# The first 100 microseconds of a hybrid decoder step: a new order of the first loads, and a written order on ACT and DVE

## The chip, the cores and the metric

The kernel runs on one core of a Trainium2 chip. The engines are TensorE (PE), VectorE (DVE), ScalarE (ACT), GpSimd (POOL) and SyncE (SP); nearly every transfer of this kernel is issued from SP's queue, in order. The metric is the device time of one execution in microseconds, the median over runs.

## The reference

One inference step of a one-layer decoder with two mixers side by side. A prompt of 2048 rows and 64 sample rows (8 sequences of 8), each 1024 wide, are normalised and projected by one weight matrix:

```python
h = rmsnorm(x, norm_w)
z = h @ w_in
q, k, v, qb, kb, vb, g_lr, gate_a, gate_b = jnp.split(z, split_points(), axis=-1)
q = rope(rmsnorm(heads(q, H_A), q_norm_w), pos)
k = rope(rmsnorm(heads(k, H_A), k_norm_w), pos)
o_a = attend(q, k, v)            # mixture of (window, dilation) = (128,1), (512,4), (2048,16)
log_a = log_sigmoid(g_lr @ w_gate_up + b_gate) / 16
o_b, s_fin = gla_chunked(qb * 64 ** -0.5, kb, vb, log_a, s0)
o_b = rmsnorm(o_b, gla_norm_w)
y = x + concat([o_a * silu(gate_a), o_b * silu(gate_b)]) @ w_out
```

8 attention heads of 64, 4 linear-attention heads. Outputs are y for prompt and sample, the new keys and values, and the final states. All inputs are float32.

## The kernel before, in words

**Numbers as pairs.** PE multiplies float16 pairs. A row tile of the prompt (128 rows) is normalised and split into a high and a low half; so is each block of weights, after scaling by powers of two. A product is then three matmuls for each of 8 slices of 128 input columns: 24 matmuls of 128x512 for each tile and block.

**The first rows.** `fetch(t)` loads x of tile t (512 KB). `prep(t)` squares it on ACT (L520), takes the inverse root with small operations on DVE and ACT (`rsqrt`, L117), writes the high half on ACT (L528) and the low half on DVE (L529), has SP transpose both by a transposing transfer (L532, into `hl`), and stores the transposed tile for later use (L536, into `h_d`). The sample rows (`prep("s")`) are transposed on PE instead (L543). Tiles 0 to 3 have input buffers of their own.

**The first weights.** `load_w(name)` is a generator. Its first step issues eight loads of 256 KB into four paired buffers of the pool `wr` (tag "wr", 4 buffers; x of tiles 4 and up uses the same tag). Eight steps take the maximum (block v: on DVE, L603; the others: a sum of squares on ACT, L608). One step brings it to a scale (`spread_max` with two small PE products, L569 and L572, then DVE). The last eight steps write the high part on ACT (L635) and the low part on DVE (L636). `between` and `behind` name rows that are fetched after half or all of the eight loads. `at_once` runs a generator to its end.

**The order.** The program calls, as traced before: fetch of the sample rows, all of `load_w("v")` with tile 0's x between its loads and tiles 1 to 3 behind, `prep("s")`, `prep(0)` to `prep(3)`; then the small tables (L1001 to L1044: `nwo` for the output weights, the masks `m3w` and `m3c`, the tables `tabs` of the two head norms with their scales `scl`); then `first(0)`. `first(0)` projects v for the sample and tiles 0 to 3, then q, then k; it calls `load_w("q")` after v's tile 0 and `load_w("k")` after v's tile 3. The projected rows are evacuated from PSUM by ACT and DVE (`post`: L736 and L744, L745 for v; L662, L663 for q and k) and, for q and k, worked on by POOL (`qk_post`, L687 to L693, with the tables of L679). Two PSUM banks (`ps_Y`) hold the sums; `vs` has two buffers (tag "z2"), `vp` one. Later blocks of rows (`first(1)` to `first(3)`) are woven with attention work. `scores_of` lists steps that read the sample's cached keys (`sample_keys`, L956) and multiply them on POOL.

**Who decides the order of an engine.** The framework records the calls and plans the order of the instructions on each engine at build time, from an estimated timeline; calls recorded earlier come first where both could run. Each engine then runs its list strictly in order. Waits for data and for buffers are added by the framework. `tc.issue_after(ins)` adds an order without a wait: each instruction recorded in the block that runs on the engine (or queue) of `ins` is placed behind `ins` in that engine's list. A buffer of a pool is given again when its last reader is done.

Of the kernel before, what the change touches and what calls it, by code (L numbers as in the profile page):

```python
# [7 lines left out]
F32 = mybir.dt.float32  # L8
# [4 lines left out]
AF = mybir.ActivationFunctionType  # L13
ALU = mybir.AluOpType
AX = mybir.AxisListType
# [3 lines left out]
P = 128  # L19
D = 1024  # L20
KT = D // P
# [12 lines left out]
Q_SCALE = 2.0**14  # L34
# [18 lines left out]
def tile_hymba(ctx: ExitStack, tc: tile.TileContext, A: dict):  # L53
# [318 lines left out]
    with ExitStack() as c1:  # L372
# [132 lines left out]
        def prep(t):  # L505
            again[0] += 1
            n = NS if t == "s" else P
            u = again[0]
            x = xs.pop(t)[:]
            wide = t != "s" and t > 3  # L510
            as_x = lambda ap: ap.rearrange("p (a c) -> p a c", a=2) if wide else ap
            if t == "s":
                hs = hps.tile([P, KT, 2 * NS], F16, name="hs")
                hi, lo = hs[:, :, 0:NS], hs[:, :, NS:]
            else:
                hl = hp.tile([P, 2, KT, n], F16, name=f"hl_{u}", tag="hl")
# [3 lines left out]
            ACT.activation(as_x(jk[:n]), x[:n], AF.Square, accum_out=ss[:n])  # L520
            rs = sm.tile([P, 1], F32, name=f"rs_{u}", tag="rs")
            rsqrt(sm, rs[:n], ss[:n], 1.0 / D, n, 1, f"x{u}", H_SCALE)
            if t != "s":
                if t < 4:
                    ht = early_ht[:, t]
                else:
                    ht = xp.tile([P, 2, D], F16, name=f"ht_{u}", tag="ht", bufs=1)[:]
                ACT.activation(as_x(ht[:, 0]), x, AF.Copy, scale=rs[:])  # L528
                DVE.scalar_tensor_tensor(  # L529
                    as_x(ht[:, 1]), x, rs[:], as_x(ht[:, 0]), ALU.mult, ALU.subtract  # L530
                )
                SP.dma_start_transpose(  # L532
                    hl[:].rearrange("p a k c -> p (a k) c"), ht.rearrange("p a c -> p (a c)")
                )
                hT[t] = (hi, lo)
                SP.dma_start(h_d[t * P : (t + 1) * P, :], hl[:].rearrange("p a k c -> p (a k c)"))  # L536
# [37 lines left out]
            )  # L574
            return pt[:, P : P + 1]

        loaded, powers = {}, {}

        def load_w(name, between=(), behind=()):

# [6 lines left out]
            for k in range(KT):  # L587
                if k % 2 == 0:
                    pair = wr.tile([P, 2, 528], F32, name=f"wr_{name}_{k}", tag="wr")
                raw = pair[:, k % 2]  # L590
                SP.dma_start(raw[:, :n], src[k * P : (k + 1) * P, c0 : c0 + n])
# [40 lines left out]
            w = wp.tile([P, 2, KT, 528], F16, name=f"w_{name}", tag="w")  # L632
            for k in range(KT):
                h, l = w[:, 0, k, :n], w[:, 1, k, :n]
                ACT.activation(h, raws[k][:, :n], AF.Copy, scale=nws[:, k : k + 1])  # L635
                DVE.scalar_tensor_tensor(  # L636
                    l, raws[k][:, :n], nws[:, k : k + 1], h, ALU.mult, ALU.subtract
                )
                yield
            loaded[name] = (w, inv)  # L640
# [2 lines left out]
        def at_once(gen):  # L643
            for _ in gen:
                pass
# [356 lines left out]
        DVE.memset(nwo[:, 0:4], 1.0)  # L1002
        for k in range(4, KT):
            SP.dma_start(nwo[:, k : k + 1], A["gla_norm_w"][0].rearrange("(k p) -> p k", p=P))
        m3w = at1.tile([P, 384], F32, name="m3w")
        SP.dma_start(m3w[:], A["c_m3"])
        m3c = at1.tile([P, 384], F32, name="m3c")
        POOL.tensor_scalar(
            m3c[:].rearrange("p (b c j) -> p b c j", c=4, j=32),
            m3w[:].rearrange("p (b j c) -> p b c j", c=4, j=32), 1e-10, None, ALU.mult,  # L1010
        )

        DVE.tensor_scalar(m3w[:], m3w[:], 1e-10, None, ALU.mult)
# [6 lines left out]
        for nm_, src in (("q", A["q_norm_w"]), ("k", A["k_norm_w"])):  # L1020
            i = "qk".index(nm_)
            w = tabs[:, 0, i]
            SP.dma_start(w, src.to_broadcast([P, 64]))
            for half in range(2):
                SP.dma_start(
                    tabs[:, 1, i, 32 * half : 32 * half + 32],
                    src[:, 32 - 32 * half : 64 - 32 * half].to_broadcast([P, 32]),
                )
            pw = scl[nm_]
            DVE.tensor_reduce(pw[:], w, AX.X, ALU.max, apply_absolute_value=True)  # L1030
            DVE.tensor_scalar(pw[:], pw[:], 2.0**-8, None, ALU.max)
            power(pw[:], pw[:])
        DVE.tensor_tensor(scl["s"][:], scl["q"][:], scl["k"][:], ALU.mult)
        DVE.tensor_scalar(scl["s"][:], scl["s"][:], -1.0 / (Q_SCALE * K_SCALE), None, ALU.mult)
        for n_, c_ in (("q", Q_SCALE), ("k", K_SCALE)):
            DVE.reciprocal(scl[n_][:], scl[n_][:])
            DVE.tensor_scalar(scl[n_][:], scl[n_][:], c_, None, ALU.mult)

        for i in range(2):
            DVE.tensor_scalar(  # L1040
                tabs[:, i, 0], tabs[:, i, 0], scl["q"][:], 0.125, ALU.mult, ALU.mult
            )
        unq = kp.tile([P, 1], F32, name="unq")
        DVE.reciprocal(unq[:], scl["q"][:])  # L1044

        kk = ap_.tile([P, NH, 4, 2, P], F16, name="kk", tag="kk", bufs=1)

# [909 lines left out]
```

## Time and profile before

| | |
|---|---|
| median of three runs | 1352.06 us (1351.25 to 1354.95) |
| the profiled execution's own time | 1347.42 us |
| its span, first to last instruction | 1345.6 us |
| mean granted TensorE clock | 0.979 |
| PE busy | 1218.3 us, 91% |
| DVE, ACT, POOL busy | 933.1, 878.8, 641.6 us |
| PE busy in 0 to 25, 25 to 60, 60 to 85 us | 3.78, 28.80, 22.65 us |
| transfers | 285.27 MB, mean 212 GB/s |
| cached keys, one load | 256.0 KB |

A row of the timeline gives start, duration, engine, line, operation, output and inputs, and the count of like instructions that it merges. In square brackets stands how long the engine had been idle before it and what ended that. A row of SPq is the issue of a transfer, not the transfer itself; when it landed is seen from who waited for it.

### The profile page before, as it was taken

What the parts mean: (1) busy time and instruction counts of PE and PEld (TensorE: products, weight loads), DVE (VectorE), ACT (ScalarE), POOL (GpSimd) and SP (SyncE); (2) the same over time, 40 slices, a digit from 0 to 9 for tenths busy, and PEclk for the clock granted to TensorE, in tenths of its full rate; (3) what the DMA queues carried; (4) which work ended last, traced back from release to release, by engine and by line L of the source; (5) the groups of instructions that cost most, each with busy time, mean ns of one, the idle gap of its engine ahead of it and who ended that gap; (6) DMA issues with size and microseconds to landing.
All of it is one profiled execution on the core that took longest, in us unless ns stands there. A gap on an engine that the chain in (4) does not pass through costs nothing.

```text
span 1345.6 us, 26148 instructions
## 1 busy us (share of the span) xinstructions
PE 1218.3 (91%) x8878; PEld 722.5 (54%) x8878; DVE 933.1 (69%) x2266; ACT 878.8 (65%) x2331; POOL 641.6 (48%) x597
## 2 busy tenths in 40 slices
PE   3798999988899798998999998789999999999998
PEld 1343565555566555665766565556655544444443
DVE  6367767788677968767771769977564387787842
ACT  5655787778568877788994557655776475465520
POOL 0076554878678645651115756777440033332310
PEclk9999999999999999999999998989999999999999
DMA  8859857778957599969886355455335768998952
GB/s 259 243 162 260 233 162 161 203 203 216 238 167 207 174 278 274 299 183 220 215 190 196 85 165 199 144 168 157 98 111 190 275 197 302 376 325 312 351 200 83
DMA packets 251721, 285.27 MB, mean 212 GB/s; under 512 B 125426, under 2 KB 160195, under 8 KB 251587
## 3 DMA queue, kind: packets, MB, share of 16 engines
q1 hardware_dynamic: 251586, 283.60, 70.7%
q8 instruction: 70, 1.15, 0.4%
q14 instruction: 65, 0.52, 0.1%
HBM read 183.12 MB, written 75.24 MB: 192 GB/s over the span
## 4 chain that ended last, share of the span: by engine, by line
PE 35%; DVE 20%; DMA 17%; POOL 10%; issue 9%; ACT 6%; SPq 3%; POOLq 0%; DVEq 0%; ACTq 0%
PE Y L1579 5%; DVE qbd L243 3%; PE acc_vb L1105 3%; PE acc_qkb L1105 3%; POOL pr L951 3%; PE acc_gb L1105 3%; PE O L467 2%; PE acc_g L1105 2%; PE s L434 2%; PE t L452 2%; DMA v<-vp_d 2%; DMA qb<-q_d 2%; PE acc_q L1105 2%; PE acc_k L1105 2%; POOL pt L419 2%
## 5 line engine op out<-in xcount | busy, mean ns | idle before, releaser
L1105 PEld LDWEIGHTS <-hr 128*128 128x128 f16 x1824 | 174.5, 99 | 133.1 <-issue 21.6
L951 POOL TENSOR_TENSOR pr<-k,qb 128x512 f32<-128x512 f32 x128 | 176.5, 1379 | 115.8 <-DVE sck L952 79.7
L445 ACT ACTIVATE p<-p,o 128x256 f32<-128x256 f32 (+1 forms) x384 | 173.2, 455 | 53.3 <-DVE o L442 49.4
L1105 PEld LDWEIGHTS <-hl 128*128 128x128 f16 x1248 | 122.4, 100 | 152.3 <-issue 26.2
L1579 PE MATMUL Y<-w_o,mh 128*128 128x512 f16 x768 | 177.5, 381 | 3.5 <-ACT mh L1538 3.4
L419 POOL TENSOR_TENSOR pt<-p,pt 128x512 f16<-128x512 f32 (+1 forms) x80 | 94.4, 1180 | 145.7 <-ACT pt L418 126.1
L1621 POOL TENSOR_TENSOR tc<-oc,w 128x512 f32<-128x512 f32 x32 | 49.0, 1550 | 178.7 <-DVE w L1613 169.5
L467 PE MATMUL O<-v,pt 128*128 128x128 f16 x1200 | 110.3, 220 | 25.1 <-DMA v<-vp_d 7.9
L1579 PEld LDWEIGHTS <-mh 128*128 128x128 f16 x768 | 71.9, 98 | 91.4 <-issue 8.8
L952 DVE TENSOR_REDUCE sck<-pr 128x8 f32<-128x512 f32 x128 | 87.0, 680 | 48.9 <-POOL pr L951 48.5
L452 PE MATMUL t<-ident,p 128*128 128x128 f32 x600 | 105.4, 279 | 5.0 <-ACT p L445 3.0
L467 PEld LDWEIGHTS <-pt 128*128 128x128 f16 x1200 | 81.9, 98 | 51.8 <-POOL pt L419 12.0
L1105 PE MATMUL acc_v<-w_v,hl 128*128 128x512 f16 x384 | 95.2, 391 | 8.5 <-DVE vp L745 3.5
L442 DVE CUSTOM_DVE_ANT_0 p<-s,m3w,scl_s 128x128 f32<-128x128 f32 (+1 forms) x256 | 89.0, 394 | 17.2 <-POOL pt L419 6.0
L1105 PE MATMUL acc_g<-w_g,hr 128*128 128x272 f16 (+1 forms) x768 | 99.2, 277 | 0.0
L1105 PE MATMUL acc_vb<-w_vb,hr 128*128 128x512 f16 x384 | 96.3, 397 | 1.4 <-ACT zg L719 1.4
L1105 PE MATMUL acc_q<-w_q,hl 128*128 128x512 f16 x384 | 93.1, 392 | 4.1 <-ACT zs_k L663 3.4
L235 ACT ACTIVATE E<-D_e 128x256 f32<-128x256 f32 (+1 forms) x168 | 67.8, 418 | 44.4 <-DVE qbd L243 16.9
L1105 PE MATMUL acc_k<-w_k,hl 128*128 128x512 f16 x384 | 91.2, 383 | 2.1 <-ACT zs_k L663 1.6
L1105 PE MATMUL acc_gb<-w_gb,hr 128*128 128x512 f16 x384 | 88.4, 385 | 3.0 <-ACT zgb L728 3.0
L434 PE MATMUL s<-kk,qq 128*128 128x256 f16 (+1 forms) x512 | 79.6, 269 | 9.5 <-DMA kk<-kp_d 4.8
L227 POOL TENSOR_TENSOR D_e<-b_e 128x512 f32<-128x512 f32 x56 | 66.4, 1196 | 23.2 <-ACT E L235 11.0
(508 smaller groups left out, 2598.2 us busy)
## 6 DMA issues: line engine op xcount, KB each, us to landing
k<-in_cache_k_win SPq DMA_DIRECT2D x104, 256.0 KB
sv<-in_cache_v_win SPq DMA_DIRECT2D x24, 1024.0 KB
hr<-h_d SPq DMA_DIRECT2D x44, 512.0 KB
qb<-q_d SPq DMA_DIRECT2D x64, 256.0 KB
o_d<-o SPq DMA_DIRECT2D x96, 132.0 KB
oc<-o_d SPq DMA_DIRECT2D x48, 264.0 KB
x<-in_x_prompt SPq DMA_DIRECT2D x16, 512.0 KB
h_d<-hl SPq DMA_DIRECT2D x16, 512.0 KB
```

Of the source, the lines that this page charges most:

```text
L227: POOL.tensor_tensor(dv, bv, bv[:, :, 0:1, B - 1 : B].to_broadcast([P, M, 2, B]), ALU.subtract)
L235: ACT.activation(ev[rows, i], dv[rows, :, half, :], AF.Exp, scale=(2 * half - 1) / 16.0)
L419: POOL.tensor_tensor(l, f, h, ALU.subtract)
L434: PE.matmul(s_ps[:, i * w : (i + 1) * w], q, k, start=(n == 0), stop=(n == len(prods) - 1),)
L442: DVE.tensor_tensor_reduce(s[:, sl], s_ps[:, sl], mask, neg, BIG, ALU.add, ALU.min, nmf(i))
L445: ACT.activation(s[:, sl], s[:, sl], AF.Exp, bias=nmf(i), scale=-1.0, accum_out=denf(i))
L452: PE.transpose(p_ps[:, i * P : (i + 1) * P], t["s"][:, i * P : (i + 1) * P], ident[:])
L467: PE.matmul(o_, t["pt"][:, c, (i * nb + b) * P : (i * nb + b + 1) * P], vf(i, b), start=(n == 0), stop=(n == 2 * nb - 1),)
L951: POOL.tensor_tensor(pr[:], kt, qt, ALU.mult)
L952: DVE.tensor_reduce(out, pr[:].rearrange("p (u k d) -> p u k d", u=2, k=4), AX.X, ALU.add)
L1105: PE.matmul(z, a_[:, k, :], w[:, p_, k, cols], start=(k == 0 and i == 0), stop=(k == KT - 1 and i == 2),)
L1579: PE.matmul(Y[:], a_[:, k, :], w_[:, part, k, :512], start=(i == 0), stop=(i == len(prods) - 1),)
```

## The change

All of it is in the first phase.

- Tile 0's x is fetched behind all eight loads of w_v, not after four of them.
- `load_w("v")` is run up to its scale; then `prep("s")` and `prep(0)` are recorded, then two of the eight weight parts, then the other six, which have to follow tile 0's halves on ACT and on DVE. `prep(1)` to `prep(3)` have to follow the last weight part on ACT and on DVE.
- The loads of w_q have to follow tile 0's transpose in SP's queue.
- The small tables are recorded after `load_w("q")`, and have to follow its last load in SP's queue. The head tables are loaded into a buffer of the pool `wr` (`tw`) and written to `tabs` by DVE (two more copies). `nwo` moves to the second block of rows, behind w_k's loads.
- The sample's cached keys are loaded behind w_k's loads.

```diff
@@ prep
-                ACT.activation(as_x(ht[:, 0]), x, AF.Copy, scale=rs[:])
-                DVE.scalar_tensor_tensor(
-                    as_x(ht[:, 1]), x, rs[:], as_x(ht[:, 0]), ALU.mult, ALU.subtract
-                )
-                SP.dma_start_transpose(
+                last["ht"] = (
+                    ACT.activation(as_x(ht[:, 0]), x, AF.Copy, scale=rs[:]).ins,
+                    DVE.scalar_tensor_tensor(
+                        as_x(ht[:, 1]), x, rs[:], as_x(ht[:, 0]), ALU.mult, ALU.subtract
+                    ).ins,
+                )
+                last["turned"] = SP.dma_start_transpose(
                     hl[:].rearrange("p a k c -> p (a k) c"), ht.rearrange("p a c -> p (a c)")
-                )
+                ).ins
@@ load_w
+                last["raw"] = SP.dma_start(raw[:, :n], src[k * P : (k + 1) * P, c0 : c0 + n]).ins
...
+                last["w"] = (
+                    ACT.activation(h, raws[k][:, :n], AF.Copy, scale=nws[:, k : k + 1]).ins,
+                    DVE.scalar_tensor_tensor(
+                        l, raws[k][:, :n], nws[:, k : k + 1], h, ALU.mult, ALU.subtract
+                    ).ins,
                 )
@@ scores_of
-                    sample_keys(*todo[i])
+                    with tc.issue_after(last["raw_k"]):
+                        sample_keys(*todo[i])
@@ the start
         fetch("s")
-        at_once(load_w("v", [0], [1, 2, 3]))
+        parts = load_w("v", (), [0, 1, 2, 3])
+        for _ in range(KT + 1):
+            next(parts)
         prep("s")
-        for t in range(4):
-            prep(t)
+        prep(0)
+        for _ in range(2):
+            next(parts)
+        with ExitStack() as rows0:
+            for i_ in last["ht"]:
+                rows0.enter_context(tc.issue_after(i_))
+            at_once(parts)
+        turned0 = last["turned"]
+        with ExitStack() as split_v:
+            for i_ in last["w"]:
+                split_v.enter_context(tc.issue_after(i_))
+            for t in range(1, 4):
+                prep(t)
...
+        def output_rows():
+            DVE.memset(nwo[:, 0:4], 1.0)
+            for k in range(4, KT):
+                SP.dma_start(nwo[:, k : k + 1], A["gla_norm_w"][0].rearrange("(k p) -> p k", p=P))
+        def mask_tables():
+            SP.dma_start(m3w[:], A["c_m3"])
...
+        def head_tables():
+            tw = wr.tile([P, 2, 528], F32, name="tw", tag="wr")[:, 0, :256].rearrange(
+                "p (s i d) -> p s i d", s=2, i=2
+            )
...
+            for i in range(2):
+                DVE.tensor_scalar(
+                    tabs[:, i, 0], tw[:, i, 0], scl["q"][:], 0.125, ALU.mult, ALU.mult
+                )
+                DVE.tensor_copy(tabs[:, i, 1], tw[:, i, 1])
+            DVE.reciprocal(unq[:], scl["q"][:])
@@ first, m == 0
                             if t == 0:
-                                at_once(load_w("q"))
+                                with tc.issue_after(turned0):
+                                    at_once(load_w("q"))
+                                with tc.issue_after(last["raw"]):
+                                    head_tables()
+                                    mask_tables()
                             elif t == 3:
                                 at_once(load_w("k", (), [4, 5, 6]))
+                                last["raw_k"] = last["raw"]
@@ first, m == 1
             if m == 1:
+                with tc.issue_after(last["raw_k"]):
+                    output_rows()
```

More of the change, by code (lines that the diff above doesn't have):

```diff
@@ L575, in spread_max @@
             return pt[:, P : P + 1]
-        loaded, powers = {}, {}
+        loaded, powers, last = {}, {}, {}
         def load_w(name, between=(), behind=()):
@@ L590, in load_w @@
                 raw = pair[:, k % 2]
-                SP.dma_start(raw[:, :n], src[k * P : (k + 1) * P, c0 : c0 + n])
+                last["raw"] = SP.dma_start(raw[:, :n], src[k * P : (k + 1) * P, c0 : c0 + n]).ins
                 raws.append(raw)
@@ L634, in load_w @@
                 h, l = w[:, 0, k, :n], w[:, 1, k, :n]
-                ACT.activation(h, raws[k][:, :n], AF.Copy, scale=nws[:, k : k + 1])
-                DVE.scalar_tensor_tensor(
-                    l, raws[k][:, :n], nws[:, k : k + 1], h, ALU.mult, ALU.subtract
+                last["w"] = (
[3 more added lines that the diff above has]
+                    ).ins,
                 )
@@ L1019, in tile_hymba @@
         scl = {n_: kp.tile([P, 1], F32, name=f"scl_{n_}") for n_ in "qks"}
[L1020 to L1027, printed above, removed]
-                )
[L1029 to L1042, printed above, removed]
@@ L1043, in tile_hymba @@
-        unq = kp.tile([P, 1], F32, name="unq")
-        DVE.reciprocal(unq[:], scl["q"][:])
+        unq = kp.tile([P, 1], F32, name="unq")
+        def output_rows():
[4 more added lines that the diff above has]
+            SP.dma_start(m3w[:], A["c_m3"])
+            POOL.tensor_scalar(
+                m3c[:].rearrange("p (b c j) -> p b c j", c=4, j=32),
+                m3w[:].rearrange("p (b j c) -> p b c j", c=4, j=32), 1e-10, None, ALU.mult,
+            )
+            DVE.tensor_scalar(m3w[:], m3w[:], 1e-10, None, ALU.mult)
@@ new lines, in head_tables @@
+        def head_tables():
+            tw = wr.tile([P, 2, 528], F32, name="tw", tag="wr")[:, 0, :256].rearrange(
+                "p (s i d) -> p s i d", s=2, i=2
+            )
+            for nm_, src in (("q", A["q_norm_w"]), ("k", A["k_norm_w"])):
+                i = "qk".index(nm_)
+                w = tw[:, 0, i]
+                SP.dma_start(w, src.to_broadcast([P, 64]))
+                for half in range(2):
+                    SP.dma_start(
+                        tw[:, 1, i, 32 * half : 32 * half + 32],
+                        src[:, 32 - 32 * half : 64 - 32 * half].to_broadcast([P, 32]),
+                    )
+                pw = scl[nm_]
+                DVE.tensor_reduce(pw[:], w, AX.X, ALU.max, apply_absolute_value=True)
+                DVE.tensor_scalar(pw[:], pw[:], 2.0**-8, None, ALU.max)
+                power(pw[:], pw[:])
+            DVE.tensor_tensor(scl["s"][:], scl["q"][:], scl["k"][:], ALU.mult)
+            DVE.tensor_scalar(scl["s"][:], scl["s"][:], -1.0 / (Q_SCALE * K_SCALE), None, ALU.mult)
+            for n_, c_ in (("q", Q_SCALE), ("k", K_SCALE)):
+                DVE.reciprocal(scl[n_][:], scl[n_][:])
+                DVE.tensor_scalar(scl[n_][:], scl[n_][:], c_, None, ALU.mult)
+            for i in range(2):
+                DVE.tensor_scalar(
+                    tabs[:, i, 0], tw[:, i, 0], scl["q"][:], 0.125, ALU.mult, ALU.mult
+                )
+                DVE.tensor_copy(tabs[:, i, 1], tw[:, i, 1])
+            DVE.reciprocal(unq[:], scl["q"][:])
```

8 lines of the change are left out of this document (removed).

## The prediction

> **What bounds the kernel now.** I read the page's busy shares first.
>
> ```profile
> PE 1218.3 (91%) x8878; PEld 722.5 (54%) x8878; DVE 933.1 (69%) x2266; ACT 878.8 (65%) x2331; POOL 641.6 (48%) x597
> ```
>
> TensorE is the bound, with 127 us idle in a span of 1345.6. The change works at the start; the table of stretches says how much is at stake there.
>
> ```profile
> 0.00:25.00 25.00, 3.78 (x14) 1.88 (x14) 14.08 (x54) 16.36 (x34) 1.98 (x8) 1.00 0.75 232
> 25.00:60.00 35.00, 28.80 (x114) 12.09 (x115) 17.93 (x38) 19.15 (x40) 0.95 (x1) 0.95 0.91 266
> 60.00:85.00 25.00, 22.65 (x98) 9.77 (x97) 12.33 (x22) 15.65 (x35) 11.06 (x18) 0.93 0.58 180
> 85.00:145.00 60.00, 52.29 (x234) 22.94 (x233) 41.78 (x65) 33.10 (x68) 44.65 (x64) 0.97 0.91 230
> ```
>
> Columns: PE, PEld, DVE, ACT, POOL busy, granted clock, DMA share, GB/s. Up to 85 us PE idles 29.8 us, 21.2 of them before 25. Next the timeline of PE: where it waits, and for what.
>
> ```profile
> 25.46 1.89 PE L1105 MATMUL acc_v<-w_v,hl 128*128 128x512 f16 x4 [0.92 <-DMA hl<-early_ht]
> 33.83 0.81 PE L779 MATMUL acc_v_s<-w_v,hs 128*128 128x512 f16 x3
> 38.15 5.35 PE L1105 MATMUL acc_v<-w_v,hl 128*128 128x512 f16 x24 [2.22 <-DMA hl<-early_ht]
> 52.73 7.03 PE L1105 MATMUL acc_v<-w_v,hl 128*128 128x512 f16 x24 [3.52 <-DVE vp L745]
> 85.19 5.34 PE L1105 MATMUL acc_k<-w_k,hl 128*128 128x512 f16 x24
> ```
>
> Tile 0 starts at 25.46 and shares PE with the sample's products (acc_v_s) until these end at 34.6; tile 1 waits for its transposed rows until 38.15, tile 3 waits until 52.73 for a PSUM bank that DVE has to empty. Then SP's queue, which issues every transfer in order, and the rows that those waits lead back to:
>
> ```profile
> 9.52 2.35 SPq L1004 DMA_DIRECT2D nwo<-in_gla_norm_w  x4
> 16.95 0.91 SPq L1025 DMA_DIRECT2D tabs<-in_k_norm_w  x2
> 19.55 3.85 SPq L532 DMA_TRANSPOSE hl<-early_ht  x1
> 24.54 0.43 SPq L964 DMA_DIRECT2D k<-in_cache_k_win  x1
> 25.91 2.71 SPq L591 DMA_DIRECT2D wr_q<-in_w_in  x4
> 29.24 2.06 SPq L591 DMA_DIRECT2D wr_q<-in_w_in  x4
> 31.69 6.67 SPq L532 DMA_TRANSPOSE hl<-early_ht  x2
> 38.46 0.53 SPq L536 DMA_DIRECT2D h_d<-hl  x1
> 39.09 3.63 SPq L532 DMA_TRANSPOSE hl<-early_ht  x1
> 46.14 0.33 SPq L536 DMA_DIRECT2D h_d<-hl  x1
> 46.52 0.46 SPq L739 DMA_DIRECT2D v_d<-vs_s  x1
> 49.88 0.69 ACT L736 ACTIVATE vs<-acc_v,wi_v 128x512 f32<-128x512 f32 x1 [8.63 <-DMA v_d<-vs_s]
> ```
>
> The third transpose stands behind the store h_d of tile 1, which waits for tile 1's landing; the last h_d waits for tile 3's, and the sample's v_d store stands behind it. ACT, holding the two z2 buffers, waits 8.63 us for that store, and PE's wait at 52.73 hangs on ACT. So tile 3 hangs on the chain of transposes, and that chain on when tile 1's rows are ready. What makes these late is on DVE and ACT:
>
> ```profile
> 9.52 1.06 ACT L520 ACTIVATE jk<-x 128x1024 bf16<-128x1024 f32 x1 [2.25 <-DMA x<-in_x_prompt]
> 14.37 1.28 DVE L529 SCALAR_TENSOR_TENSOR early_ht<-x,rs,early_ht 128x1024 f16<-128x1024 f32 x1 [0.20 <-ACT early_ht L528]
> 16.47 0.23 DVE L630 TENSOR_SCALAR ns_v<-nw,pr_v 128x8 f32<-128x8 f32 x1
> 18.17 5.00 ACT L635 ACTIVATE w_v<-wr_v,ns_v 128x512 f16<-128x512 f32 x8
> 21.79 0.22 DVE L1030 TENSOR_REDUCE scl_k<-tabs 128x1 f32<-128x64 f32 x1 [3.94 <-DMA tabs<-in_k_norm_w]
> 26.41 2.92 DVE L636 SCALAR_TENSOR_TENSOR w_v<-wr_v,ns_v,w_v 128x512 f16<-128x512 f32 x4
> 29.26 1.27 DVE L529 SCALAR_TENSOR_TENSOR early_ht<-x,rs,early_ht 128x1024 f16<-128x1024 f32 x1
> ```
>
> Tile 0's rows are split by 15.65 (14.37 and 1.28), yet their transpose is issued at 19.55, behind the tables and a cache load. DVE stands still 3.94 us on a table that nothing needs soon, with the low parts of w_v queued behind it; these end at 29.33, and only then comes tile 1's low half (30.53).
>
> **The change part by part.** *First loads.* Tile 0's x moves behind the last four weights. The list of transfers:
>
> ```profile
> GB/s 27 179 378 390 405 415 113 7 167 244 288 354 360 370 233 222 277 297 179 301 186 221 254 176 270 334 116 152 46 285 167 105 117 204 295 376 89 79 157 67
> wr_v<-in_w_in SPq DMA_DIRECT2D x8, 256.0 KB
> ```
>
> Slices are 2.5 us. Four times 256 KB (1.05 MB) at about 390 GB/s is 2.7 us: tile 0's square starts at 12.2 instead of 9.52. From that start to the end of its low half took 6.13 us, so it is split at 18.3. Its x (0.52 MB) no longer precedes the last weights, which come 1.3 us sooner; with DVE's 1.28 for tile 0 out of the middle of the scale's chain as well, the scale (done at 16.70) comes at 14.1 to 15.4. I take 14.8.
>
> *Tables behind w_q, and cache loads behind w_k.* From SP's queue ahead of the first transpose go ten table loads, the mask and the cache loads, and from DVE the wait of 3.94. So the transpose goes out when the rows are ready, 18.3, not 19.55: 1.25 us. DVE's two new table copies are 64 columns on each of two tables, below the 0.73 of a weight part, off the path.
>
> *The written order.* ACT: weight parts 0 and 1 (5.00/8 = 0.63 each) from 14.8 to 16.1, tile 0's high half, then parts 2 to 7 until about 21.0. DVE: tile 0's low half until 18.3 or 18.6, then six low parts at 2.92/4 = 0.73: 23.0 instead of 29.33. What waits behind the last part, by the new order, is tile 1's square on ACT. With tile 0's 6.13 us from square to low half, its rows are ready at 27.1 (before 30.53). SP: w_q's loads stay behind the first transpose (18.3 + 3.85 = 22.2) and took 5.4 us to issue, until 27.6. So tile 1's transpose goes out at about 27.3, not 31.69: **-4.4 us**. The sample's sixteen products now run ahead of tile 0; that gain is hidden, as tile 1 waits for the transpose (27.3 + the 6.5 from 31.69 to 38.15 = 33.8). Tile 3's start hangs on the same chain, so all of it moves by 4.4.
>
> *Transfers out of the way.* Four cache loads of 256 KB leave the window of the first transposes. Later ones, with less beside them, took:
>
> ```profile
> 101.21 2.35 SPq L532 DMA_TRANSPOSE hl<-ht  x1
> 105.77 0.34 SPq L536 DMA_DIRECT2D h_d<-hl  x1
> ```
>
> 4.6 us from issue to landing, against 5.9 at 19.55. Bounds 0 and -1.3; w_q's loads still run beside tile 1's, so I take -0.5.
>
> *Stores.* With w_v whole at 23, the sample's product is done some ten us sooner than at 34.6, and its store may leave SP before the transposes. Then the wait of 8.63 on ACT goes; next is the store vp_d of tile 0, whose tile has one buffer, and which in the old order still stands behind the last h_d. Bounds: 0, and the 3.52 wait with the 1.7 by which tile 3's products run slower after it (7.03 against 5.34), -5.2. Nearest is the old order: -1.5.
>
> The Trainium skill, TensorE: Matmul & The Clock Gate, Part 1, says that an idle window of about 3.4 us drops the array to half rate. Here tile 0 would end two to five us before tile 1's rows land; by that rule tile 1 pays 1.7 as well, and the sum would be -3.7. I leave it out, since after the 2.22 us wait at 38.15 the 24 products took a warm 5.35.
>
> *The tables' new place.* The tables take a buffer of the weights' pool, so they wait for w_q's first pair, and w_k's last pair waits for them.
>
> ```profile
> 52.59 5.39 DVE L636 SCALAR_TENSOR_TENSOR w_q<-wr_q,ns_q,w_q 128x512 f16<-128x512 f32 x8
> 54.04 0.81 SPq L591 DMA_DIRECT2D wr_k<-in_w_in  x2
> 57.24 2.90 SPq L591 DMA_DIRECT2D wr_k<-in_w_in  x6
> 61.02 0.72 ACT L608 ACTIVATE jw_k<-wr_k,nw 128x512 bf16<-128x512 f32 x1 [2.11 <-DMA wr_k<-in_w_in]
> 66.54 0.27 PE L569 MATMUL mx_k<-ident,w_k 128*1 128x128 f32 x1 [1.61 <-DVE w_k L616]
> 81.92 3.39 DVE L636 SCALAR_TENSOR_TENSOR w_k<-wr_k,ns_k,w_k 128x512 f16<-128x512 f32 x5
> 68.07 1.26 POOL L687 TENSOR_TENSOR t_q<-zs_q,ct_q 128x512 f32<-128x512 f32 x1 [40.61 <-ACT zs_q L663]
> ```
>
> Before: first pair free at 54.0, w_k's last load issued at 60 and landed by 64 (3.8 us, as from 57.24 to 61.02). After, on the same clock: tables issued 54.0 to 57, landed 4.8 later at the latest (the old loads: issued from 16.95, used at 21.79), so by 61.8; some nine small dependent operations like the 0.22 of scl_k bring DVE to 63.7; then the last pair is issued and landed at 67.5: 3.5 us later than now. PE already waits 1.61 for this maximum, and w_k's last low part ends at 85.31, when PE starts on k: no slack in this row. But between the maximum and the parts lie eleven us of queueing, which can absorb it. Bounds 0 and +3.5; I take +1.0. The tables themselves are needed at 68.07, so their own landing is covered. The mask is first needed by the attention, behind k's four tiles. The loads of nwo (2.35 us of SP) move into the second block of rows; with W_out far off I cost them at nothing; uncovered they cost those 2.35.
>
> **Sum:** -4.4 - 0.5 - 1.5 + 1.0 = -5.4 us, about the unit of change that a measurement here can tell (0.3% is 4 us). POOL's dense stretch (44.65 of the 60 us from 85 on) starts at 68.07, when q's first tile is evacuated, and so moves along; from there on each wait is on other work, not on a clock time. The profiled run took 1347.42 (1345.6 and 1.8 around it), 4.6 below the median: 1342.0 on it, **1346.7** on the median.
>
> **The rivals.** *w_k paces.* The +3.5 counts in full and the stores stay: -4.4 + 3.5 = -0.9, 1351.2, no change. For: no slack at 85.19. Against: the eleven us of queueing.
>
> *The stores go first.* -4.4 - 5.2 - 0.5 = -10.1, 1342. For: the sample's product comes early. Against: vp_d's single buffer.
>
> *The tables' wait moves into w_q's parts: slower.* Orders on an engine are fixed from an estimate. In the old one scl_k stood ahead of all low parts of w_v while its load took 4.8 us. If it now stands ahead of w_q's parts 2 to 7, DVE waits up to 4.8 with q's weights behind it, and w_k's last pair adds 3.5: 8.3 - 4.4 = +3.9, and with the scale of w_k late by the same wait up to another 1 or 2: some +5, 1357. It decides once the tables' waits exceed 4.4 + 4 = 8.4 us. Against: the tables can't be issued before w_q's first pair is split, which the estimate knows too. The Trainium skill, DMA: Bandwidth & Descriptors, Rules for kernel authors, speaks for it: issue a transfer early and wait on it late, which for the tables is undone here.
>
> **How the numbers follow.** Forecast 0.46, stores first 0.12, w_k paces 0.26, tables' wait 0.16. The forecast's own range is 1343 to 1348.5; small parts of it fall short of 4 us. So faster 0.56, same 0.28, slower 0.16. The range runs from 1341, the stores' case with its upper bound of 1.3 for the transfers, to 1355.5, short of the slower case; it leaves out most of that case and the faster tail, under 2 in 10.
>
> **What would show it.** After: first transpose issued near 18, w_v's last part near 23, tile 1's products near 34, tile 3's near 47, k's near 80. DVE's 3.94 wait gone; if one of like size stands among w_q's parts, the slower rival has it. Wrong is all of this if the first block ends sooner but PE's idle time between 85 and 400 grows by as much: the order of every engine is planned anew, and nothing in this trace bounds that.

## The result, and the profile after: slower by 1.1%

| | before | after |
|---|---|---|
| median | 1351.65 us (1350.92 to 1354.95) | 1366.58 us (1364.15 to 1370.85) |
| the profiled execution, its span | 1347.42, 1345.6 us | 1365.44, 1363.6 us |
| mean granted TensorE clock | 0.979 | 0.974 |

The ratio is 1.0113, with a 95% interval of 1.0083 to 1.0143: 15 us slower, where 5.4 us faster was forecast. The table of stretches of the changed kernel (columns as in the prediction):

```profile
0.00:25.00 25.00, 8.79 (x30) 3.85 (x31) 15.77 (x43) 14.70 (x29) 0.45 (x7) 1.00 0.78 243
25.00:60.00 35.00, 23.64 (x98) 9.96 (x97) 14.08 (x33) 20.33 (x43) 1.53 (x1) 0.90 0.74 194
60.00:85.00 25.00, 21.15 (x90) 9.29 (x90) 9.85 (x32) 12.00 (x30) 9.76 (x19) 0.86 0.71 238
85.00:145.00 60.00, 47.45 (x194) 19.85 (x193) 39.81 (x62) 31.84 (x66) 35.47 (x56) 0.91 0.71 189
```

The first 25 us are better: PE has done 30 matmuls, not 14. By 60 us the lead is gone (126 against 128), by 145 us PE has done 408, against 457. From 60 us on its clock was granted at 0.86 and 0.91, where it had been 0.93 and 0.97. POOL did 35.47 us of work in the last stretch instead of 44.65. So the loss lies between 25 and 145 us. The timeline of PE in the changed kernel:

```profile
22.56 3.43 PE L1130 MATMUL acc_v<-w_v,hl 128*128 128x512 f16 x13 [0.17 <-DMA hl<-early_ht]
35.74 6.65 PE L1130 MATMUL acc_v<-w_v,hl 128*128 128x512 f16 x19 [5.86 <-DVE w_q L618]
50.41 5.34 PE L1130 MATMUL acc_v<-w_v,hl 128*128 128x512 f16 x24 [1.25 <-DVE vp L749]
63.85 12.49 PE L1130 MATMUL acc_q<-w_q,hl 128*128 128x512 f16 x48 [8.10 <-DVE scl_k L564]
76.18 0.27 PE L571 MATMUL mx_k<-ident,w_k 128*1 128x128 f32 x1
80.92 0.38 PE L574 MATMUL mx_k<-mm_k,ident 1*128 1x1 f32 x2
89.16 0.81 PE L1130 MATMUL acc_k<-w_k,hl 128*128 128x512 f16 x3 [1.50 <-DVE w_k L639]
105.04 12.21 PE L1130 MATMUL acc_k<-w_k,hl 128*128 128x512 f16 x48 [3.15 <-ACT zs_k L667]
123.32 8.30 PE L1130 MATMUL acc_v<-w_v,hl 128*128 128x512 f16 x24 [6.07 <-DMA hl<-ht]
157.68 0.61 PE L434 MATMUL s<-kk,qq 128*128 128x128 f16 x8
```

v's tiles 0, 1 and 3 start 2.9, 2.4 and 2.3 us sooner than at 25.46, 38.15 and 52.73. Then q's first tile waits 8.10 us and starts 4.3 us later than before (59.59). `mx_k` is the name of two small products that turn w_k's maxima into its scale. The first comes at 76.18, where before had it at 66.54, the second at 80.92, where before had it at 73.86. k's first tile (its first product is at 87.29) runs at the pace at which DVE writes w_k's low parts; and the first attention scores (`s`, L434) start at 157.68. In before the second product, w_k's high parts and the scores were:

```profile
73.86 0.38 PE L572 MATMUL mx_k<-mm_k,ident 1*128 1x1 f32 x2
76.70 5.00 ACT L635 ACTIVATE w_k<-wr_k,ns_k 128x512 f16<-128x512 f32 x8
144.87 0.61 PE L434 MATMUL s<-kk,qq 128*128 128x128 f16 x8 [0.51 <-DMA kk<-kp_d]
```

So 12.8 of the 15 us are lost before the first scores, and most of it late: k's first product is only 2.1 us behind (before: 85.19). Rows of the other engines of the changed kernel that lead there:

```profile
18.12 1.90 SPq L534 DMA_TRANSPOSE hl<-early_ht  x1
18.01 5.39 DVE L639 SCALAR_TENSOR_TENSOR w_v<-wr_v,ns_v,w_v 128x512 f16<-128x512 f32 x8
21.58 1.05 ACT L520 ACTIVATE jk<-x 128x1024 bf16<-128x1024 f32 x1
24.79 0.72 ACT L610 ACTIVATE jw_q<-wr_q,nw 128x512 bf16<-128x512 f32 x1
28.38 1.14 ACT L529 ACTIVATE early_ht<-x,rs 128x1024 f16<-128x1024 f32 x1
30.86 6.37 SPq L534 DMA_TRANSPOSE hl<-early_ht  x2
58.11 0.22 DVE L1055 TENSOR_REDUCE scl_q<-tw 128x1 f32<-128x64 f32 x1 [2.30 <-DMA tw<-in_q_norm_w]
60.39 0.22 DVE L1055 TENSOR_REDUCE scl_k<-tw 128x1 f32<-128x64 f32 x1 [0.68 <-DMA tw<-in_k_norm_w]
62.94 0.20 DVE L1068 COPY tabs<-tw 128x64 f32<-128x64 f32 x1 [1.51 <-DMA tw<-in_k_norm_w]
63.12 0.68 DVE L749 SCALAR_TENSOR_TENSOR vp<-acc_v,vp 128x512 f16<-128x512 f32 x1
63.83 0.33 SPq L750 DMA_DIRECT2D vp_d<-vp  x1
64.19 2.25 SPq L593 DMA_DIRECT2D wr_k<-in_w_in  x4
86.53 5.00 ACT L638 ACTIVATE w_k<-wr_k,ns_k 128x512 f16<-128x512 f32 x8
```

DVE waits 4.49 us (2.30 + 0.68 + 1.51) for the tables among w_q's low parts, and the evacuation of v's tile 2 (`vp`, 63.12) stands behind; when it ends at 63.80, q's first tile starts. In SP's queue the store of that pair (`vp_d`, 63.83) stands ahead of w_k's last four loads, which are issued from 64.19 to 66.44; before, all eight had been issued by 60.14. w_k's high parts follow at 86.53, 9.8 us later than before.

### The profile page after: what moved, and what is told of

Its sections match the earlier page's. It is cut to its first block, busy times and chain, and to the rows that moved or that the text cites. A ratio compares the mean times of both kernels' runs of the same rounds, so it can differ in the third digit from the quotient of the medians.

```text
span 1363.6 us, 26146 instructions
## 1 busy us (share of the span) xinstructions
PE 1223.3 (90%) x8878; PEld 726.4 (53%) x8878; DVE 934.8 (69%) x2268; ACT 880.5 (65%) x2331; POOL 638.1 (47%) x597
## 4 chain that ended last, share of the span: by engine, by line
PE 33%; DVE 20%; DMA 15%; issue 13%; POOL 11%; ACT 6%; SPq 3%; POOLq 0%; DVEq 0%; ACTq 0%
PE Y L1611 4%; PE acc_vb L1130 4%; DVE qbd L243 3%; POOL pr L955 3%; PE acc_g L1130 3%; PE acc_gb L1130 3%; DMA qb<-q_d 2%; PE acc_qkb L1130 2%; PE acc_v L1130 2%; PE acc_q L1130 2%; PE O L467 2%; POOL pt L419 2%; PE t L452 2%; PE s L434 2%; DMA T_q<-qp_d 1%
## 5 line engine op out<-in xcount | busy, mean ns | idle before, releaser
L1130 PE MATMUL acc_vb<-w_vb,hr 128*128 128x512 f16 x384 | 93.1, 386 | 3.3 <-ACT zg L723 3.3
L434 PE MATMUL s<-kk,qq 128*128 128x256 f16 (+1 forms) x512 | 79.4, 270 | 7.9 <-DVE o L442 5.7
L452 PEld LDWEIGHTS t<-ident,p 128*128 128x128 f32 x600 | 68.6, 143 | 20.8 <-ACT p L445 11.8
```

What stands on the lines that cost most here:

```text
L434: PE.matmul(s_ps[:, i * w : (i + 1) * w], q, k, start=(n == 0), stop=(n == len(prods) - 1),)
L452: PE.transpose(p_ps[:, i * P : (i + 1) * P], t["s"][:, i * P : (i + 1) * P], ident[:])
L1130: PE.matmul(z, a_[:, k, :], w[:, p_, k, cols], start=(k == 0 and i == 0), stop=(k == KT - 1 and i == 2),)
```

## The experiments

The column "scores" is the start of the first attention scores, "mx_k" that of its first product on PE, both from the profile of that run (mx_k and scores in us). A ratio is to the kernel before, run on the same chip.

| kernel | mx_k | scores | ratio, interval |
|---|---|---|---|
| before | 66.54 | 144.87 | 1 |
| after | 76.18 | 157.68 | 1.0113 (1.0083 to 1.0143) |
| own | 72.79 | 154.00 | 1.0051 (1.0029 to 1.0072) |
| rows_only | 72.82 | 149.94 | 1.0033 (1.0017 to 1.0048) |
| tables_only | 73.30 | 149.52 | 1.0046 (1.0029 to 1.0063) |
| slot_only | 77.91 | 162.28 | 1.0123 (1.0097 to 1.015) |
| before_late | 71.99 | 148.63 | 1.0024 (1.0005 to 1.0043) |
| mx_rows | 67.33 | 145.54 | 1.0008 (0.999 to 1.0027) |
| mx_own | 69.31 | 148.43 | 1.0030 (1.0009 to 1.0052) |
| mx_after | 70.52 | 149.84 | 1.0029 (1.0011 to 1.0047) |
| keys_only | 71.91 | 148.50 | 1.0033 (1.0012 to 1.0053) |
| mx_keys | 67.64 | 143.46 | 1.0005 (0.9988 to 1.0022) |
| rf_rows | 63.77 | 140.69 | 0.9992 (0.9969 to 1.0014) |
| rf_own | 65.54 | 144.36 | 1.0007 (0.9987 to 1.0026) |
| t1_own | 66.56 | 146.02 | 1.0014 (0.9993 to 1.0034) |
| t1_after | 66.48 | 145.25 | 1.0000 (0.9982 to 1.0018) |

Over these sixteen kernels, 1 us at the first scores goes with 0.90 us of time (ratio less 1, times 1352), with a correlation of 0.97. So the start of the scores is a fair measure of what an edit costs. The work behind the scores took 1200.7 to 1209.3 us in the single profiled runs (span less scores; before and `slot_only` at one end, `t1_own` at the other), a scatter in which the kernels stand in no order of their edits; so the place to look is ahead of the scores.

**Which half of the change: the tables or the start?** Theory A put the loss on the tables in the weights' buffer, theory B on the first loads and the written order. `own` keeps everything but loads the tables straight to their place:

```diff
-            tw = wr.tile([P, 2, 528], F32, name="tw", tag="wr")[:, 0, :256].rearrange(...)
-                w = tw[:, 0, i]
+                w = tabs[:, 0, i]
```

> The changed kernel, but the head tables are loaded straight into their own tile (as in the kernel before), so they take no buffer of the weights' pool and can be loaded as soon as w_q's loads are issued. Theory A (the tables in the weights' buffer cost the time: DVE stands still for them among w_q's low parts, and w_k's last pair waits for them): the 8.1 us wait of PE before q is gone, w_k's last low part ends near 83 to 86 instead of 97, tile 4's v starts near 108 to 112 instead of 123, and the time is 1347 to 1352, 2 to 5 us under the kernel before at best, since tile 3 started 2.3 us earlier. Theory B (the first loads and the written order on ACT and DVE cost it, through what is planned behind them): the time stays at 1360 or more.

`rows_only` is `own` with tables, masks and output rows at their old place:

```diff
-                                with tc.issue_after(last["raw"]):
-                                    head_tables()
-                                    mask_tables()
@@ ahead of first(0)
+        output_rows()
+        mask_tables()
+        head_tables()
```

> The changed kernel with the tables, masks and output rows put back where they were before (own tiles, behind the first four tiles' rows): what is left of the change is the order of the first loads, the written order on ACT and DVE, w_q's loads behind tile 0's transpose and the cached keys behind w_k. Theory A: no loss, 1347 to 1353, with DVE's wait for the tables back among w_v's low parts, 2 to 4 us. Theory B: 1360 or more.

`tables_only` is the kernel before with nothing but the tables moved:

```diff
-        parts = load_w("v", (), [0, 1, 2, 3])
...
+        at_once(load_w("v", [0], [1, 2, 3]))
+        prep("s")
+        for t in range(4):
+            prep(t)
```

> The kernel before with the tables alone moved as in the change (head tables through a buffer of the weights' pool behind w_q, mask behind them, output rows in the second block); first loads, order of ACT and DVE and cached keys as before. Theory A: the whole loss and more, as the start's 2.3 us are not won: 1364 to 1372. Theory B: 1350 to 1354.

`slot_only` is `own` with a buffer of `wr` taken and filled by six small loads that nothing reads:

```diff
                                     mask_tables()
+                                    tw = wr.tile([P, 2, 528], F32, name="tw", tag="wr")[:, 0, :384]
+                                    for i_, src_ in enumerate((A["q_norm_w"], A["k_norm_w"])):
+                                        for j_ in range(3):
+                                            o_ = 192 * i_ + 64 * j_
+                                            SP.dma_start(
+                                                tw[:, o_ : o_ + 64], src_.to_broadcast([P, 64]))
```

> The kernel 'own' with one unused buffer of the weights' pool between w_q and w_k, filled by six small loads like the tables': w_k's last pair waits for a slot as in the change, but DVE waits for no table. If the late w_k carries theory A's loss: w_k's maximum is taken 2 to 4 us later than in 'own', w_k's last low part 4 to 10 us later, time 1356 to 1362. If DVE's stand among w_q's parts carries it: within 2 us of 'own'. Theory B has no view on the difference.

Neither theory held. `own` (1359.92 us) came out next to B's 1360; `rows_only` (1354.88) and `tables_only` (1357.22) lie between the two, so each half alone made the kernel slower, by 0.3 to 0.5%. `slot_only` reproduces the changed kernel (1.0123) without the wait of DVE among w_q's parts:

```profile
53.97 5.39 DVE L639 SCALAR_TENSOR_TENSOR w_q<-wr_q,ns_q,w_q 128x512 f16<-128x512 f32 x8 [0.79 <-ACT w_q L638]
```

So that wait is not needed for the loss. `slot_only` also exceeded what either half of its expectation gave. What the four share is the second column: the first product of mx_k is 6 to 11 us late in all.

**Theory C: the place of mx_k in PE's order.** Before runs q's tile 0, then the first product of mx_k, then 21 products of tile 1, then the second. In `own`, `rows_only` and `tables_only` 19 or 20 of tile 1's 24 products stand ahead of the first, in the changed kernel and in `slot_only` all 24. In these the second follows 21 or 22 products later. The scale needs both, and the second comes 3.7 us later than before in `own` and `rows_only` (77.53, 77.55), 8.8 us later in `slot_only` (82.64). `before_late` puts mx_k behind 18 products in the kernel before, with nothing of the change in it. Its edit also records w_k's scale and parts at that place, so it moves a little more than mx_k:

```diff
-                                at_once(load_w("k", (), [4, 5, 6]))
+                                parts_k = load_w("k", (), [4, 5, 6])
+                                for _ in range(KT):
+                                    next(parts_k)
...
+                        if (name, t) == ("q", 1):
+                            q1 = project(name, [t])
+                            for _ in range(6):
+                                next(q1)
+                                yield
+                            with tc.issue_after(lastmm[0]):
+                                at_once(parts_k)
+                            yield from q1
```

> The kernel before with one thing moved: the product that finds w_k's largest value (mx_k) is put behind 18 of the 24 products of tile 1's q, where own, rows_only and tables_only have it, instead of ahead of them; nothing of the change is in it. Theory C (what the variants lose after k's first tile comes from mx_k standing one tile of q later on PE: w_k's scale, its sixteen parts, the x fetches that wait for its buffers and the qp store behind those all come some 4 us later): k's first tile stays near 85 us, tile 4's v goes from 110.4 to 114.5-117.5, first scores near 149, time 1355 to 1360. Theory D (the loss is scatter of the order that is planned behind the first tiles, whatever the place of mx_k): within 1.5 us of the time before, tile 4's v within 1.5 us of 110.4.

`mx_rows`, `mx_own` and `mx_after` do the opposite: tile 1's q products have to follow mx_k on PE, the first 21 its first product, the last three its second.

```diff
                             with ExitStack() as behind_mx:
+                                if (name, t) == ("q", 1):
+                                    behind_mx.enter_context(
+                                        tc.issue_after(mxk["mx1" if k < KT - 1 else "mx2"]))
```

> rows_only (1354.9; the new load order and written order with tables and masks at their old place) with tile 1's q products held behind mx_k on PE, as the kernel before has them. Theory C: from k's first tile to tile 4's v 25-27 us instead of 30.9, time 1348 to 1352. Theory D: 1353.5 to 1356.5, the stretch stays near 31.

> own (1359.9; the whole change with the tables loaded straight to their place, no buffer of the weights' pool) with tile 1's q products held behind mx_k. Theory C: from k's first tile to tile 4's v 25-29 us instead of 35.0, time 1351 to 1355.5. Theory D: 1358 to 1362.

> The changed kernel (1366.6) with tile 1's q products held behind mx_k; the tables still pass through a buffer of the weights' pool. w_k's squares end only at 71.4 us there, so PE would wait some 2.4 us for mx_k after q's first tile. Theory C: mx_k at 71.6 instead of 76.2, w_k's parts some 4 us earlier, so products of k no longer at the pace of its low parts: 1358 to 1363, still above own with the same edit because the late w_k stays. Theory D: within 2 us of 1366.6. If the wait for the buffer alone makes the whole loss: no gain, 1366 to 1369.

The stretches are C's: from k's first tile to tile 4's v it is 25.6 us in `mx_rows` and 27.8 in `mx_own`, and `before_late` has tile 4's v at 115.18. The times are less clear. `before_late` (1355.70 us; 1.0024, and 3.8 us at the scores) and `mx_own` (1355.18) lie in C's range, `mx_after` (1356.67) below it, and `mx_rows` (1353.69) in D's. The edge took `rows_only` from 1.0033 to 1.0008 and `own` from 1.0051 to 1.0030, steps whose intervals overlap, and the changed kernel from 1.0113 to 1.0029: 0.84%, or 11.4 us, clear of the noise and more than the 4 to 9 expected. In `mx_after` PE still waits 7.58 us ahead of q; what has moved is mx_k:

```profile
62.53 7.97 PE L1135 MATMUL acc_q<-w_q,hl 128*128 128x512 f16 x24 [7.58 <-DVE scl_k L564]
70.52 0.27 PE L571 MATMUL mx_k<-ident,w_k 128*1 128x128 f32 x1
```

With the edge, the change with the tables in the weights' buffer (1.0029) and without it (1.0030) are alike: once mx_k is in its place, no cost of the buffer is seen, within some 0.3%.

**How little tips it.** `keys_only` is the kernel before with the cached keys' loads behind w_k's, the smallest part of the change; `mx_keys` adds the edge.

```diff
-                    sample_keys(*todo[i])
+                    with tc.issue_after(last["raw_k"]):
+                        sample_keys(*todo[i])
```

> The kernel before with the smallest part of the change alone: the loads of the cached keys stand behind w_k's loads on SP. Its built order puts mx_k behind 19 of tile 1's 24 q products on PE, where before has it ahead of them. Theory C (the place of mx_k carries the loss, whichever edit tips it): first transpose some 1 us earlier or the same, w_k's eight high parts near 81 instead of 76.7, first attention scores at 147-150 instead of 144.9, 1354 to 1358 against 1351-1352 of before (ratio 1.002 to 1.005). Theory H (each part of the change costs or gains by what it moves): four small loads that are needed late leave the queue of the start, so the same or up to 1 us faster.

> keys_only with tile 1's q products held behind mx_k on PE. Theory C: the loss of keys_only is gone, ratio to before 0.998 to 1.001, first scores at 143.5 to 145.5. Theory H: as keys_only, the edge by itself being worth nothing.

Both are in C's range: +0.33% and +0.05%, though the two intervals overlap. An edit lets the framework plan all that stands behind it anew, so one such pair could be chance, as theory D has it; but all five pairs moved the way of C (`before` to `before_late`, and the edge on four kernels). The timelines of `keys_only`, with its stretch from 85 to 112 us:

```profile
71.91 0.27 PE L569 MATMUL mx_k<-ident,w_k 128*1 128x128 f32 x1
80.05 5.00 ACT L635 ACTIVATE w_k<-wr_k,ns_k 128x512 f16<-128x512 f32 x8
83.48 4.51 SPq L501 DMA_DIRECT2D x<-in_x_prompt  x4
83.87 4.48 PE L1106 MATMUL acc_k<-w_k,hl 128*128 128x512 f16 x20
86.42 0.40 POOL L133 TENSOR_TENSOR ra_q<-rr_q 128x8 f32<-128x8 f32 x1 [3.58 <-ACT rr_q L125]
88.05 0.58 SPq L771 DMA_DIRECT2D qp_d<-qp  x1
93.82 0.63 ACT L769 ACTIVATE qp<-t_q 128x512 f16<-128x512 f32 x1 [1.42 <-DMA qp_d<-qp]
106.79 6.99 PE L1106 MATMUL acc_k<-w_k,hl 128*128 128x512 f16 x24 [3.84 <-ACT zs_k L663]
85.00:112.00 27.00, 20.11 (x85) 8.55 (x84) 17.59 (x32) 14.44 (x36) 18.84 (x35) 0.94 0.79 205
```

then of `mx_keys`:

```profile
67.64 0.27 PE L569 MATMUL mx_k<-ident,w_k 128*1 128x128 f32 x1 [0.82 <-DVE w_k L616]
76.22 5.01 ACT L635 ACTIVATE w_k<-wr_k,ns_k 128x512 f16<-128x512 f32 x8 [0.89 <-DVE ns_k L630]
79.35 0.63 SPq L501 DMA_DIRECT2D x<-in_x_prompt  x1
83.70 4.48 PE L1111 MATMUL acc_k<-w_k,hl 128*128 128x512 f16 x20
102.07 5.34 PE L1111 MATMUL acc_k<-w_k,hl 128*128 128x512 f16 x24 [1.10 <-ACT zs_k L663]
85.00:112.00 27.00, 22.78 (x104) 10.07 (x103) 18.24 (x32) 17.00 (x38) 24.55 (x41) 1.00 0.77 198
```

and the same stretch of before:

```profile
85.00:112.00 27.00, 23.15 (x106) 10.22 (x105) 18.51 (x30) 15.93 (x36) 24.19 (x39) 1.00 0.76 199
```

k's first tile starts at the same time in both (83.87 and 83.70), so in `keys_only` w_k itself is not late for PE. What is late is the rest. w_k's eight high parts, 5 us on ACT, stand 3.8 us later, between q's small operations; POOL waits 3.58 us for one of these. The x of the next tiles need w_k's buffers, so all four (2 MB) go out in one burst from 83.48, right ahead of a q store, and ACT waits 1.42 us for that store, until 93.82. POOL, which before keeps busy (24.19 of 27 us in this stretch), loses 5 to 6 us. PE's waits for ACT to evacuate k's tiles grow with it: 1.83 and 3.84 us ahead of the third and fourth tile, where `mx_keys` has 0.63 and 1.10. That the one leads to the other is read from the order of the rows. Which of the two, the block on ACT or the burst, carries more was not separated.

**Does the start gain anything once this is out of the way?** `rf_rows` and `rf_own` add a second edge to `mx_rows` and `mx_own`: rows 2 and 3 and w_q's squares behind row 1 on ACT.

```diff
+            prep(1)
+            ht1 = last["ht"][0]
+            with tc.issue_after(ht1):
+                for t in (2, 3):
+                    prep(t)
...
-                                with tc.issue_after(turned0):
+                                with tc.issue_after(turned0), tc.issue_after(ht1):
                                     at_once(load_w("q"))
```

> mx_rows with tile 1's row work set ahead on ACT: the squares of rows 2 and 3 and all of w_q's squares stand behind the high half of row 1 (in the changed kernel ten of them ran ahead of it, and the transpose was issued at 30.9 instead of the predicted 27.3). Theory F (the start sets the end: what tile 1 gains is passed on): tile 1's products at 33-35 instead of 38, and the time some 3 us below mx_rows, ratio to before 0.997 to 0.999. Theory G (what the first tiles gain is taken up before k's first tile, by the stores of v's pairs and w_k's loads and squares): tile 1's products as early, but k's first tile still within 1 us of 85.9 and the ratio 0.999 to 1.002.

> The same two edits (tile 1's row work ahead on ACT, tile 1's q products behind mx_k) on own, that is the whole change with the tables loaded straight to their place. DVE has no table work among w_v's low parts here, so tile 1's transpose should be issued near 27.4 and its products start near 32 instead of 38.5. Theory F: 4-6 us below mx_own, ratio to before 0.998 to 1.000. Theory G: k's first tile within 1 us of 85.4, ratio 1.001 to 1.004 as mx_own had.

Both came out about 0.2% below the kernel without the second edge (1.0008 to 0.9992, 1.0030 to 1.0007), a step within the noise, and neither can be told from the kernel before. `rf_rows` has tile 1's products at 34.88, k's first tile at 79.83 and the scores 4.2 us ahead of before, so theory G's account of the start fell there, but F's 3 us of time were not shown and the ratio lies in G's range. In `rf_own` the transpose went out at 31.57, not 27.4, and tile 1's products started at 35.85; k's first tile, at 81.60, was again earlier than G had it. `t1_own` and `t1_after` put the tables' loads behind that transpose on SP, the latter with the whole change:

```diff
-                                with tc.issue_after(last["raw"]):
+                                with tc.issue_after(turned1):
                                     head_tables()
                                     mask_tables()
```

> rf_own with the tables' and masks' loads behind tile 1's transpose on SP (in rf_own row 1 was ready at 27.2 us, and its transpose stood behind seven small loads until 31.57). Expected: that transpose issued at 27.3-28, tile 1's products at 31.8-33 instead of 35.9, first scores at 139 to 142 instead of 144.4. Theory F (what the start gains reaches the end): ratio to before 0.995 to 0.998, 1345 to 1349. Theory J (the work behind the first scores gives the gain back): scores as early, ratio 0.999 to 1.002.

> The changed kernel with all its parts, the tables in the weights' buffer among them, and three order edits: tile 1's q products behind mx_k, rows 2 and 3 and w_q's squares behind row 1 on ACT, the tables' loads behind tile 1's transpose on SP. Transpose of tile 1 near 27.5, its products near 32. If the buffer by itself costs little (theory C), first scores at 141-146 instead of mx_after's 149.8, ratio 0.998 to 1.001. If the buffer costs what slot_only seemed to show, DVE's wait among w_q's low parts and w_k's late pair hold the first scores at 148-151 and the ratio stays at 1.002 to 1.004.

`t1_after`, the change as it stands with three order edges, takes the time of the kernel before (1.0000), and its scores (145.25) are where theory C had them. `t1_own` had its transpose (27.06) and tile 1's products (32.65) as expected, but missed behind them: 1.0014, where F had 0.995 to 0.998, and its scores came at 146.02, not 139 to 142, 1.7 us later than `rf_own`'s. The timeline of `t1_after` says where the gain goes:

```profile
27.29 3.17 SPq L534 DMA_TRANSPOSE hl<-early_ht  x1
32.50 6.86 PE L1138 MATMUL acc_v<-w_v,hl 128*128 128x512 f16 x24 [3.09 <-DMA hl<-early_ht]
35.13 2.18 ACT L529 ACTIVATE early_ht<-x,rs 128x1024 f16<-128x1024 f32 x2
39.12 5.48 SPq L534 DMA_TRANSPOSE hl<-early_ht  x2
44.48 12.86 PE L1138 MATMUL acc_v<-w_v,hl 128*128 128x512 f16 x48 [4.27 <-DMA hl<-early_ht]
59.80 6.85 PE L1138 MATMUL acc_q<-w_q,hl 128*128 128x512 f16 x24 [2.45 <-DVE vp L749]
```

Tile 1 starts at 32.50, 5.65 us ahead of before. But rows 2 and 3 stand behind six squares of w_q on ACT: their high halves are written from 35.13 to 37.3, their low halves end at 38.8, their transposes are issued at 39.12, tile 2 waits 4.27 us, and q's first tile starts at 59.80, in before at 59.59. Nothing is left of tile 1's gain there. No kernel here beats the one before by more than the measurement can tell; `rf_rows` comes nearest.

## Why the prediction was wrong, step by step

- **First loads, the written order up to tile 0: right.** First transpose issued at 18.12 (forecast 18.3), w_v's last low part ended at 23.4 (23.0), DVE's 3.94 gone.
- **Tile 1's transpose, -4.4: the first step that failed is "its rows are ready at 27.1".** It carried tile 0's 6.13 us over to row 1, though behind w_v's parts ACT has other work: the squares of rows 2 and 3 and four of w_q's came between row 1's square (21.58) and its high half (28.38). Issued at 30.86, the gain was 0.8. With ACT's and SP's orders mended it was 27.06 (`t1_own`) and 27.29 (`t1_after`), as forecast.
- **"Tile 3's start hangs on the same chain, so all of it moves by 4.4": wrong too.** `t1_after` shows the gain used up by rows 2 and 3. What is late next was not looked for on ACT.
- **Transfers -0.5, stores -1.5: too small.** The first transpose took 4.4 us to land (18.12 to 22.56, where PE follows with 0.17 of wait), below the 4.6 of the better bound; tile 1's products started 4.88 us after the issue of theirs (30.86 to 35.74), where before it was 6.46. ACT still waited 6.80 us for the store v_d (before 8.63), but PE's wait ahead of tile 3 fell from 3.52 to 1.25, and that tile took 5.34 us, not 7.03. In all, v's tile 3 ended 4.0 us sooner (55.75 against 59.76), of the 6.4 that these two terms and the -4.4 give.
- **The tables' place, +1.0 of a bound of +3.5: the step that turned a gain into a loss.** The wait stands where the slower rival put it, among w_q's parts, at 4.49 us, below the 8.4 from which that rival was to decide. q's first tile started 4.3 us later than before, so 8.3 us were lost between v's tile 3 and q. `slot_only` and `mx_after` show that this wait does not carry the loss in the end. The buffer does, through mx_k: in `own`, without it, 19 products stand ahead of mx_k, in the changed kernel and in `slot_only` 24. That the plan did so because w_k's loads come later there was not tested. "Eleven us of queueing, which can absorb it" was read as slack; it absorbed nothing (10.2 us from mx_k to w_k's parts before, 66.54 to 76.70; 10.4 after, 76.18 to 86.53).
- **What no term held:** where the plan puts the instructions behind the start. The text named this as what could overturn it and gave it no price. The place of mx_k was 11.4 of the 15.3 us (0.0113 of 1352), by `mx_after`. PE's idle time between 85 and 400 us did grow, by 7.6 us: PE was busy 47.45 instead of 52.29 us from 85 to 145, and 232.50 instead of 235.22 from 145 to 400. But the block ahead of it did not end sooner, as that sentence supposed: k's products started at 87.29, where 80 was forecast and before had 85.19. The other 3.9 us (1.0029 to 1.0000) go with the further edges of `t1_after`; what they are spent on stays open.
- **The clock rule left out.** The Trainium skill, TensorE: Matmul & The Clock Gate, Part 1, has the array drop to half rate after an idle window of about 3.4 us. The term of 1.7 was due: in the changed kernel tile 1 waited 5.86 us and its first 19 products took 6.65, where 19 took 4.26 in `mx_keys` after a wait of 2.70. In `t1_after` tile 1 took 6.86 after a wait of 3.09, 1.5 us more than the 5.35 before, and that wait was shorter than the rule's figure.

## What to carry to other kernels

Where engines run a planned order, a change at the start can be paid for by where the plan puts small instructions behind it. List the short operations that many others hang on (here two products of 0.27 and 0.38 us that give a block of weights its scale), and pin them with an order edge before judging the rest. A transfer moved out of the way is not free if it tips such a place: here four loads moved cost 0.33%, and with one edge 0.05% was left. And a gain at one tile counts only as far as the next tile's inputs are early as well.

## What the runs showed of the hardware

The same 24 products of 128x512 take 5.34 us or 6.8 to 8.3, by the wait ahead of them. In the sixteen traces 89 unbroken rows of 24 with a wait ahead start between 20 and 130 us. Each of the 47 with a wait of 1.93 us or less took 5.34 us. Of the 27 with 2.81 or more, 26 took 6.82 or longer and one took 5.34 (`tables_only`, at 125.31, after 3.16). Of the 15 between 1.99 and 2.73, nine took 6.85 to 7.03 and six 5.34 or 5.35. Two rows of like wait, the first of `mx_keys`, the second of `keys_only`:

```profile
59.80 7.03 PE L1111 MATMUL acc_q<-w_q,hl 128*128 128x512 f16 x24 [2.73 <-DVE vp L745]
```

```profile
60.08 5.34 PE L1106 MATMUL acc_q<-w_q,hl 128*128 128x512 f16 x24 [2.73 <-DVE vp L745]
```

The granted clock differs with them: in `mx_keys` it was 0.64 from 59.8 to 61.8 us, 0.51 from 61.8 to 63.8 and then 1.00; in `keys_only` it was 1.00 from 60.1 to 64. So a wait of 2 us can already cost PE 1.7 us more, and between 2 and 3.2 us the length of the wait alone does not say whether it will.
